# The last down product as seven block products, its weight sums made by paced DMAs

## The chip, the cores and the metric

The kernel runs on one core of a Trainium2 chip. The metric is the device time of one execution in microseconds (us). Three runs of the kernel before gave 3523.32, 3526.65 and 3530.71 us; the median is 3526.65 us. All times below are of this kernel before the change.

## The reference

Three transformer blocks run one after the other on a sequence of 1024 positions with 1024 features, all in fp32. Each block has a mixing part and a feed-forward part (f1, f2, f3 below). What matters here is the feed-forward part of the third block and what stands around it:

```python
mod = jax.nn.silu(c) @ w_ada + b_ada          # six vectors of 1024: shifts, scales, gates
x = x + gate1 * rms_norm_3(mix, norm1_post)   # mix: spatial gating and pools, times w_out
h = rms_norm_3(x, norm2_pre) * (1.0 + scale2) + shift2
f = jnp.square(jax.nn.relu(h @ w_fc1)) @ w_fc2   # 1024 -> 4096 -> 1024
x = x + gate2 * rms_norm_3(f, norm2_post)
```

`f` is a product of 1024 x 4096 activations with a 4096 x 1024 weight. It is called the down product of f3.

## The kernel before, in words

Activations lie feature-major: `X[half]` holds 8 tiles of 128 features by 512 positions, for two halves of the positions. Every product of a weight tile with an activation tile is three TensorE matmuls (`mm3`), since both operands are split into a high part and a remainder (`hi`/`lo`, `Hh`/`Hl`): high by high, high by low, low by high. The high part is written by ScalarE (`whi<-raw`, `Hh<-raw`), the remainder by VectorE (`wlo<-raw,whi`, `Hl<-raw,Hh`).

The weights come as one stream (`Stream`): `load` (L183) issues a DMA of up to 512 KB on SyncE's queue into one of the `raw` buffers, `_split` makes high part and remainder of it in a slot, and the products take the slots in the order of the stream. `tick` is called after every few matmuls; it splits the next weight when its load is old enough by the kernel's own count of matmul time (`self.pe`).

The up products (`up7`) already use Strassen's scheme with seven products (in Winograd's form). Their results go through `relu2` on ScalarE and by a DMA on its queue to a DRAM tensor `gdf`. `start` fetches one of the seven partial results back by a DMA on GpSimd's queue.

The down product of f3 (`down7`) goes over the 4096 hidden features in nine chunks of two or four tiles of 128 (`CHUNKS`). For each chunk and each of 8 output tiles and 2 halves it accumulates in PSUM, and VectorE adds the sum to `X` (`X<-X,mm`). The last chunk works in pieces of 512, 256 and 256 positions (`PARTS`). Then `tail` takes the mean of squares (`ax<-ones,acc`), spreads the reciprocal root over the partitions by a small matmul (`row_bcast`: `ax<-ident,rr`), scales (`X<-X,gp,ax`), adds the residual `xr` and sends the result out.

What stands between the products runs as background generators next to them: the norm after f2 (`norm2_gen`), the pools of block 3 (`ax<-w,wpl`, a chain of four window sizes, each built from the one before by GpSimd's shift-and-add on `w`), spatial gating (`ax<-ws,vg`), the norm after the output product o3 (`post`, then `norm_gen`), and the vectors of `mod`. For each of their 48 columns `ada_unit` (L634) forms products of `w_ada` and `silu(c)` by eight VectorE instructions, and `ada_flush` sums them over the partitions with a matmul `ax<-ones,ada`.

Two things set the order. The Python code emits instructions with these generators stepped by `self.pe`. Then the Tile framework schedules them when the program is built: each engine gets one fixed list, from an estimate of what is ready when. On the chip each engine goes through its list in that order; an instruction whose operands are not there holds back those behind it on the same engine.

Of the kernel before, what the change touches and what calls it, by code (L numbers as in the profile page):

```python
# [57 lines left out]

def _feat(a):

    return np.ascontiguousarray(a.T.reshape(KT, P, a.shape[0]).transpose(1, 0, 2))


def lay_out(i):
# [42 lines left out]
    a["w3_down"] = i["w_fc2_3"].reshape(32, P, D)  # L107
# [40 lines left out]
class Stream:  # L148
# [5 lines left out]
    def __init__(self, k):  # L154
# [6 lines left out]
        self.raws = []  # L161
        self.groom = [False, False]
# [40 lines left out]
    def _split(self):  # L203
# [38 lines left out]
        while self.nd < min(self.ns + 2, len(self.seq)):  # L242
# [23 lines left out]


class Kern:
    def __init__(self, tc, a, out):
# [7 lines left out]
        self.adap = None  # L277

# [44 lines left out]
    def mm(self, out, l, r, s, e, grp=False):  # L323
        self.nc.tensor.matmul(out, l, r, start=s, stop=e, skip_group_check=grp)  # L324
# [326 lines left out]

    CHUNKS = {"f1": [2, 2] + [4] * 7, "f2": [2] + [4] * 5, "f3": [2, 2] + [4] * 7}

# [4 lines left out]
    def setup(self):  # L658
# [46 lines left out]
        def ffn7(n, up, down, with_ada=0):  # L705
# [19 lines left out]
            S[n + "h"], S[n + "d"] = [], []  # L725
            gd = S[n + "x"] = self.drp.tile([a[down].shape[0], P, T], F32, name="gd" + n)
# [168 lines left out]
    def up7(self, name):  # L895
# [3 lines left out]
        gated = name == "f2"  # L899
# [7 lines left out]
        def relu2(dst, src, m, t, scale=1.0):  # L907
            self.act(dst, src, AF.Relu, scale=scale)
            self.act(dst, dst, AF.Square)
            nc.scalar.dma_start(out=gd[m, :, 512 * t:512 * t + 512], in_=dst)  # L910
# [12 lines left out]
        for g in range(0, M, 2):  # L923
# [7 lines left out]
            for i in (0, 1):  # L931
# [7 lines left out]
                else:  # L939
                    relu2(s, ps[i], 2 * (g + i), 0)  # L940
# [7 lines left out]
        def slot():  # L948
            n[0] += 1
            return X1[:, (n[0] - 1) % 8]  # L950
# [6 lines left out]
        def start(g):  # L957

            ca = wide() if gated else None
            s1 = None  # L960
            if g < M:
                s1 = scratch() if gated else slot()
                nc.gpsimd.dma_start(out=s1, in_=sd[g])
                if gated:
                    nc.gpsimd.dma_start(out=ca[:, :512], in_=cd[g])
            return s1, ca

        nxt = start(0)
        for g, G in enumerate(groups):
# [18 lines left out]
            if g >= M:  # L988
# [4 lines left out]
                else:  # L993
                    relu2(slot(), z, 2 * g, 0)
# [11 lines left out]
            if not gated:  # L1006
                relu2(c22, c22, 2 * g + 1, 1)
# [4 lines left out]
            else:  # L1012
                relu2(c21, c21, 2 * g + 1, 0)
# [9 lines left out]
            else:  # L1023
                relu2(v, v, 2 * g, 1)
        W.groom[1] = True
        self.ext_es.close()
        self.open_ss()

    def down7(self, name, add, tail, quarters=False):
# [4 lines left out]
        residual = 0 if name == "f3" else 4  # L1034
# [478 lines left out]
    def block2(self):  # L1513
# [243 lines left out]

        self.up7("f2")
# [268 lines left out]
    def block3(self):  # L2027
# [204 lines left out]
        self.hp, e = self.pool("hp2", 1, None, "right")  # L2232
        self.ffn_es.insert(0, e)
        ac = []

        def add(m, part, ps, first, last):
            half, c0, c1 = part
            o = c0 - half * 512
            x = self.X[half][:, m, o:o + c1 - c0]
            if first:  # L2240
# [84 lines left out]
```

## Time and profile before

| | |
|---|---|
| time, median of 3 | 3526.65 us (3523.32 to 3530.71) |
| profiled execution | 3526.44 us |
| its span | 3524.6 us |
| TensorE clock granted, mean share | 0.983 |
| PE busy | 3419.4 us (97%), 16725 instructions |
| VectorE / ScalarE / GpSimd busy | 62% / 39% / 10% |
| DMA | 421.46 MB, mean 120 GB/s |

PE is TensorE, DVE VectorE, ACT ScalarE, POOL GpSimd, SP SyncE. The span is from the first to the last instruction of the profiled execution; 1.84 us of that execution lie around it. A row such as "L324 MATMUL mm<-Hh,whi" names the line of the helper, the operation, the tile written and the tiles read. PE, at 97%, is the engine whose idle stretches are to be looked for.

### The profile page before, as it was taken

What the parts mean: (1) busy time and instruction counts of PE and PEld (TensorE: products, weight loads), DVE (VectorE), ACT (ScalarE), POOL (GpSimd) and SP (SyncE); (2) the same over time, 40 slices, a digit from 0 to 9 for tenths busy, and PEclk for the clock granted to TensorE, in tenths of its full rate; (3) what the DMA queues carried; (4) which work ended last, traced back from release to release, by engine and by line L of the source; (5) the groups of instructions that cost most, each with busy time, mean ns of one, the idle gap of its engine ahead of it and who ended that gap; (6) DMA issues with size and microseconds to landing.
All of it is one profiled execution on the core that took longest, in us unless ns stands there. A gap on an engine that the chain in (4) does not pass through costs nothing. (4 is left out here: it accounts for less than half of the span.)

```text
span 3524.6 us, 43683 instructions
## 1 busy us (share of the span) xinstructions
PE 3419.4 (97%) x16725; PEld 2808.1 (80%) x16725; DVE 2201.8 (62%) x3747; ACT 1367.4 (39%) x2046; POOL 335.8 (10%) x368
## 2 busy tenths in 40 slices
PE   7999999999999989999999999999999999999998
PEld 7788898887888777876698788878778878877887
DVE  5456366556666574667768988867665676645444
ACT  3432244444112443555634444431332564451111
POOL 0111020000000210000020000000232410000003
PEclk9999999999999999998999999999999999999999
DMA  3111444336633186444325322274222154343222
GB/s 106 48 43 47 148 135 148 117 118 191 184 133 113 58 196 173 123 129 147 110 94 166 116 84 84 96 221 149 88 67 90 62 184 149 132 167 114 96 84 72
DMA packets 180964, 421.46 MB, mean 120 GB/s; under 512 B 18088, under 2 KB 58744, under 8 KB 180628
## 3 DMA queue, kind: packets, MB, share of 16 engines
q1 hardware_dynamic: 133044, 325.34, 28.8%
q10 hardware_dynamic: 38304, 67.13, 5.1%
q0 software_dynamic: 9408, 26.22, 3.6%
q8 instruction: 131, 2.15, 0.3%
q14 instruction: 77, 0.63, 0.1%
HBM read 304.50 MB, written 105.63 MB: 116 GB/s over the span
## 5 line engine op out<-in xcount | busy, mean ns | idle before, releaser
L324 PE MATMUL mm<-Hh,whi 128*128 128x512 f32 (+3 forms) x3632 | 1384.2, 381 | 11.7 <-DVE X L305 4.5
L324 PE MATMUL mm<-Hh,wlo 128*128 128x512 f32 (+3 forms) x3632 | 1365.6, 377 | 4.7 <-DVE wlo L305 4.7
L324 PE MATMUL mm<-Hl,whi 128*128 128x512 f32 (+3 forms) x3632 | 1369.6, 377 | 0.2 <-DVE Hl L305 0.2
L324 PEld LDWEIGHTS mm<-Hh,whi 128*128 128x128 f32 x3632 | 686.0, 189 | 155.3 <-issue 6.8
L324 PEld LDWEIGHTS mm<-Hh,wlo 128*128 128x128 f32 x3632 | 685.7, 189 | 138.5 <-DVE wlo L305 9.0
L324 PEld LDWEIGHTS mm<-Hl,whi 128*128 128x128 f32 x3632 | 686.1, 189 | 127.7 <-issue 1.4
L319 ACT ACTIVATE whi<-raw 128x1024 fp32r<-128x1024 f32 (+3 forms) x386 | 379.0, 992 | 694.6 <-PE mm L324 459.9
L305 DVE TENSOR_TENSOR wlo<-raw,whi 128x1024 fp32r<-128x1024 f32 (+3 forms) x386 | 441.7, 1151 | 193.3 <-ACT whi L319 182.8
L305 DVE TENSOR_TENSOR X<-X,mm 128x512 f32<-128x512 f32 (+1 forms) x446 | 290.3, 655 | 366.7 <-PE mm L324 362.1
L324 PE MATMUL mm<-t,whi 128*128 128x512 f32 x1296 | 408.6, 396 | 2.4 <-ACT whi L319 2.4
L324 PEld LDWEIGHTS mm<-t,whi 128*128 128x128 f32 x1296 | 242.9, 188 | 62.4 <-ACT whi L319 3.3
L324 PE MATMUL mm<-t,wlo 128*128 128x512 f32 x648 | 256.7, 396 | 1.9 <-DVE wlo L305 1.7
L319 ACT ACTIVATE Hh<-raw 128x1024 fp32r<-128x1024 f32 x86 | 89.6, 1057 | 364.8 <-PE mm L324 213.3
L321 ACT ACTIVATE X<-X 128x512 f32<-128x512 f32 (+1 forms) x226 | 151.9, 673 | 186.2 <-DVE X L310 153.7
L305 POOL TENSOR_TENSOR acc<-acc,sq 128x256 f32<-128x256 f32 (+1 forms) x108 | 115.9, 1074 | 910.0 <-ACT sq L321 906.4
L305 DVE TENSOR_TENSOR raw<-raw 128x512 f32<-128x512 f32 x216 | 145.2, 687 | 79.5 <-DMA raw<-in_w_up 77.1
L324 PEld LDWEIGHTS mm<-t,wlo 128*128 128x128 f32 x648 | 121.8, 188 | 33.4 <-DVE wlo L305 4.1
L305 DVE TENSOR_TENSOR Hl<-raw,Hh 128x1024 fp32r<-128x1024 f32 x86 | 104.6, 1222 | 56.9 <-ACT Hh L319 56.3
L310 DVE SCALAR_TENSOR_TENSOR ada<-raw,silc,ada 128x128 f32<-128x128 f32 x336 | 115.5, 350 | 8.3
L324 PE MATMUL mm<-whi,Hh 128*128 128x264 f32 (+4 forms) x336 | 111.7, 342 | 6.5 <-ACT Hh L319 2.8
L324 PE MATMUL mm<-wlo,Hh 128*128 128x264 f32 (+4 forms) x336 | 111.2, 340 | 2.4 <-DVE wlo L305 2.4
L310 DVE SCALAR_TENSOR_TENSOR X<-mm,X 128x512 f32<-128x512 f32 x108 | 74.5, 690 | 61.6 <-PE mm L324 60.1
(290 smaller groups left out, 3400.0 us busy)
## 6 DMA issues: line engine op xcount, KB each, us to landing
raw<-in_w_up SPq DMA_DIRECT2D x136, 512.0 KB
raw<-gdf SPq DMA_DIRECT2D x86, 512.0 KB
raw<-in_w_down SPq DMA_DIRECT2D x86, 512.0 KB
gdf<-X ACTq DMA_DIRECT2D x108, 256.0 KB
raw<-in_w_ada SPq DMA_DIRECT2D x48, 512.0 KB
gdf<-X ACTq DMA_DIRECT2D x22, 512.0 KB
B<-qd SPq DMA_DIRECT2D x36, 256.0 KB
A<-qd SPq DMA_DIRECT2D x36, 256.0 KB
```

Source lines behind the costliest of these rows:

```text
L305: eng.tensor_tensor(out=out, in0=a, in1=b, op=op)
L310: self.nc.vector.scalar_tensor_tensor(out=out, in0=a, scalar=s, in1=b, op0=op0, op1=op1)
L319: self.nc.scalar.activation(out, in_, f, scale=scale, **kw)
L321: self.nc.scalar.activation(out, in_, f, bias=bias, scale=scale, **kw)
L324: self.nc.tensor.matmul(out, l, r, start=s, stop=e, skip_group_check=grp)
```

## The change

The rows and columns of f3's down weight are laid out as blocks (four groups of hidden features, by four quarters of the matrix, `_quarters`). The 4096 x 1024 weight and the hidden activations are cut into 2 x 2 blocks, and the product is made of seven block products of 512 x 2048 x 512 instead of eight (`down_parts`). Four of the seven need sums of weight blocks. These are made in DRAM, by 32 DMAs of 1 MB on GpSimd's queue: 16 plain copies into `sw` and 16 that add to it (`sums`). They are spread out from the start of the up product of f2 (`up7("f2")`) by a pace of 24.0 on `self.pe`. Each waits for the last matmul that the source has emitted before it. The up product of f3 writes the seven pieces of the hidden activations that the products need: four more VectorE operations and four DMA writes on GpSimd's queue per group. The weight stream of the down product gets both operands of each product from DRAM; the residual `xr` comes in by two GpSimd DMAs into `Hh` at its start. The last part of `tail` is one of 512 positions.

The core of the diff:

```diff
     def tick(self):
         self.k.ada_flush()
+        self.k.sums_step()
     def mm(self, out, l, r, s, e, grp=False):
-        self.nc.tensor.matmul(out, l, r, start=s, stop=e, skip_group_check=grp)
+        self.last_mm = self.nc.tensor.matmul(out, l, r, start=s, stop=e, skip_group_check=grp)
+    def sums(self, name, w, pace, at=None):
+        S = self.S[name + "s"]
+        for i, q in ((0, 1), (1, 0), (2, 1), (3, 2)):
+            for e in range(4):
+                self.sums_todo.append((S[i, 2 * e:2 * e + 2], w[e, q], {}))
+        for i, q in ((0, 3), (1, None), (2, 0), (3, None)):
+            for e in range(4):
+                r = slice(2 * e, 2 * e + 2)
+                src = w[e, q] if q is not None else S[i - 1 if i == 1 else 1, r]
+                self.sums_todo.append((S[i, r], src, dict(accum_op=ALU.add, max_dma_last_dim=4096)))
+    def sums_step(self):
+        if self.sums_todo and self.pe >= self.sums_at:
+            dst, src, kw = self.sums_todo.pop(0)
+            ins = self.nc.gpsimd.dma_start(out=dst, in_=src, **kw)
+            self.tc.add_manual_dep(
+                ins.ins, self.last_mm.ins.name,
+                mybir.DependencyInfo(mybir.DependencyClass.Sync, mybir.DependencyReason.DATA),
+                reason="sums")
+            self.sums_at = self.pe + self.sums_pace
+    ORDER = ("P1", "P2", "P6", "P7", "P4", "P5", "P3")
...
+    def down_parts(self, name, out, tail):
+        W.ahead = 4
+        for n, i in enumerate(self.ORDER):
+            if new:
+                ps = [self.ps() for _ in range(4)]
+            for e in range(8):
+                wa, wb = (W.get(u) for u in D_[8 * n + e])
+                for m in range(4):
+                    for k in (0, 1):
+                        self.mm3(ps[m], wa.hi[:, w], wa.lo[:, w], wb.hi[:, x], wb.lo[:, x], ...)
...
+        self.sums("f3", a["w3_down"], 24.0)
         self.up7("f2")
...
+                if parts:
+                    relu2(v, v)
+                    t1_, t2_, t4_ = slot(), slot(), slot()
+                    self.tt(t1_, ca, v, ALU.subtract)
+                    self.tt(v, c22, v, ALU.subtract)
+                    self.stt(t2_, t1_, -1.0, c22, ALU.mult, ALU.subtract)
+                    self.stt(t4_, t2_, -1.0, c21, ALU.mult, ALU.subtract)
+                    for i, t in ((3, t1_), (5, v), (4, t2_), (6, t4_)):
+                        nc.gpsimd.dma_start(out=piece(i, g), in_=t)
...
+        xr = self.Hh.bitcast(F32)
+        for k in (0, 4):
+            nc.gpsimd.dma_start(out=xr[:, k:k + 4, :T], in_=self.xd[:, k:k + 4])
...
-        self.down7("f3", add, tail, quarters=True)
+        self.down_parts("f3", out, tail)
```

With the 32 DMAs in the program the framework arrives at other lists, also where the source is the same. Three places follow, all on TensorE; numbers behind a name tell tiles apart.

In the down product of f2 the five sums of columns of `mod` stood apart, with 36 to 84 matmuls between each and the next (here the first of them):

```order
L324 MATMUL mm_19031<-Hl_87,whi_18935 128x512
L324 MATMUL mm_19031<-Hh_86,wlo_18936 128x512
L324 MATMUL ax_19045<-ones_60,ada_18959 128x1
L324 MATMUL mm_19052<-Hh_86,whi_18804 128x512
L324 MATMUL mm_19052<-Hl_87,whi_18804 128x512
L324 MATMUL mm_19052<-Hh_86,wlo_18805 128x512
```

Now the five stand in a row, ahead of 24 matmuls that the first of them stood behind (`mm_19026` is the `mm_19006` of before):

```order
L337 MATMUL mm_19008<-Hl_87,whi_18954 128x512
L337 MATMUL mm_19008<-Hh_86,wlo_18955 128x512
L337 MATMUL ax_19065<-ones_60,ada_18979 128x1
L337 MATMUL ax_19129<-ones_60,ada_19040 128x1
L337 MATMUL ax_19197<-ones_60,ada_19104 128x1
L337 MATMUL ax_19243<-ones_60,ada_19172 128x1
L337 MATMUL ax_19386<-ones_60,ada_19300 128x1
L337 MATMUL mm_19026<-Hh_86,whi_18823 128x512
L337 MATMUL mm_19026<-Hl_87,whi_18823 128x512
```

The fifth sum, which had 192 matmuls between the first and itself, now stands ahead of all of them.

In the third block's pools, each window's products (`wpl`, from buffer `w0` or `w1`) had 60 to 84 matmuls of another product between them and those of the next window; here is the second window:

```order
L324 MATMUL mm_20966<-Hl_87,whi_20844 128x512
L324 MATMUL mm_20966<-Hh_86,wlo_20845 128x512
L324 MATMUL ax_20979<-w0_20738,wpl_20740 128x512
L324 MATMUL ax_20982<-w0_20738,wpl_20740 128x512
L324 MATMUL mm_20966<-Hh_86,whi_20844 128x512
```

Now they stand behind that whole product, with 12 matmuls from the second window to the third (shown) and 12 from the third to the fourth:

```order
L337 MATMUL ax_21008<-w0_20765,wpl_20767 128x512
L337 MATMUL mm_21422<-Hh_86,whi_21135 128x512
L337 MATMUL mm_21444<-Hh_86,whi_21217 128x512
L337 MATMUL mm_21466<-Hh_86,whi_21301 128x512
L337 MATMUL mm_21422<-Hl_87,whi_21135 128x512
L337 MATMUL mm_21422<-Hh_86,wlo_21136 128x512
L337 MATMUL mm_21444<-Hl_87,whi_21217 128x512
L337 MATMUL mm_21444<-Hh_86,wlo_21218 128x512
L337 MATMUL mm_21466<-Hl_87,whi_21301 128x512
L337 MATMUL mm_21466<-Hh_86,wlo_21302 128x512
L337 MATMUL mm_21489<-Hh_86,whi_21405 128x512
L337 MATMUL mm_21489<-Hl_87,whi_21405 128x512
```

The rest of the twelve is one more matmul, and then come the products of the third window.

At the end of the output product o3, the sums and broadcasts of the norms stood between its matmuls, from here on:

```order
L324 MATMUL mm_21782<-Hl_87,whi_21678 128x256
L324 MATMUL mm_21782<-Hh_86,wlo_21679 128x256
L324 MATMUL ax_21795<-ones_60,acc_21508 128x1 x4
L324 MATMUL mm_21782<-Hh_86,whi_21678 128x256
L324 MATMUL mm_21782<-Hl_87,whi_21678 128x256
```

Now they stand behind o3's last matmul (`mm_22437`), and ahead of the first of f3's up product (`mm_22500`):

```order
L337 MATMUL mm_22437<-Hh_86,wlo_21712 128x256
L337 MATMUL ax_21828<-ones_60,acc_21540 128x1 x4
L337 MATMUL ax_21903<-ones_60,acc_21540 128x1 x4
L337 MATMUL ax_21871<-ident_59,rr_21836 128x128 x2
L337 MATMUL ax_21984<-ident_59,rr_21911 128x128 x2
L337 MATMUL ax_22037<-ones_60,acc_21540 128x1 x4
L337 MATMUL ax_22119<-ident_59,rr_22045 128x128 x2
L337 MATMUL ax_22166<-ones_60,acc_21540 128x1 x4
L337 MATMUL ax_22301<-ones_60,acc_21669 128x1 x4
L337 MATMUL ax_22249<-ident_59,rr_22174 128x128 x2
L337 MATMUL mm_22500<-Hh_86,whi_22236 128x512
```

The nine `ax` groups are the post norm and the next norm of the first half of the positions, in two parts, and the first sums of the second half; some 300 matmuls of o3 moved ahead of them.

At the end of f2's down product, likewise, the norm's broadcast (`ax<-ident,rr`), which stood 32 matmuls behind its sums (`ax<-ones,acc`), now follows them directly, and the first matmuls of the next product follow it.

## Rows read from the trace of the kernel before

**Rows 1.** The page: busy time, share of the span and instructions.
```profile
PE 3419.4 (97%) x16725; PEld 2808.1 (80%) x16725; DVE 2201.8 (62%) x3747; ACT 1367.4 (39%) x2046; POOL 335.8 (10%) x368
```
**Rows 2.** Busy time by stretch: columns named in its second row, of f3.
```profile
core 0: us, PE busy (x) PEld busy (x) DVE busy (x) ACT busy (x) POOL busy (x), PEclk, DMA share, GB/s
2890.00:3160.00 270.00, 267.97 (x1150) 215.29 (x1149) 153.39 (x199) 128.89 (x184) 4.31 (x8) 1.00 0.44 149
3160.00:3200.00 40.00, 38.76 (x166) 30.46 (x165) 26.51 (x31) 16.84 (x20) 0.00 (x0) 1.00 0.53 175
3200.00:3450.00 250.00, 250.00 (x1079) 202.07 (x1078) 108.29 (x132) 41.85 (x41) 0.00 (x0) 1.00 0.26 85
...
3150.00:3155.00 5.00, 5.00 (x22) 3.75 (x20) 0.00 (x0) 0.40 (x1) 0.00 (x0) 1.00 1.04 413
```
**Rows 3.** Costliest groups, f3's down product: count | busy us, mean ns | idle before.
```profile
L305 DVE TENSOR_TENSOR X<-X,mm 128x512 f32<-128x512 f32 x90 | 61.4, 686 | 128.6 <-PE mm L324 128.6
L305 DVE TENSOR_TENSOR wlo<-raw,whi 128x1024 fp32r<-128x1024 f32 x22 | 26.5, 1223 | 5.8 <-ACT whi L319 5.8
```
**Rows 4.** The page's costliest groups, f3's up product.
```profile
L310 DVE SCALAR_TENSOR_TENSOR X<-mm,X 128x512 f32<-128x512 f32 x108 | 74.5, 690 | 61.6 <-PE mm L324 60.1
```
**Rows 5.** DMA issues: KB each, median us to landing.
```profile
X<-xd POOLq DMA_DIRECT2D x8, 1024.0 KB, 13.7
```
**Rows 6.** The timeline, end of f3: start, length, instruction, idle before it.
```profile
3495.77 1.30 POOL L305 TENSOR_TENSOR X<-X,xr 128x512 f32<-128x512 f32 x1
3509.51 0.73 POOL L305 TENSOR_TENSOR X<-X,xr 128x256 f32<-128x256 f32 x1 [0.63 <-DVE X L310]
3520.37 0.44 DVE L305 TENSOR_TENSOR X<-X,xr 128x256 f32<-128x256 f32 x1
```
**Rows 7.** The timeline, f2's down product, PE, SP and DVE.
```profile
2373.44 0.28 PE L324 MATMUL ax<-ones,ada 128*128 128x1 f32 x2
2385.76 0.33 SPq L183 DMA_DIRECT2D raw<-in_w_ada  x1
2390.30 0.28 DVE L314 TENSOR_SCALAR ada<-raw,silc 128x128 f32<-128x128 f32 x1
2393.02 0.73 DVE L310 SCALAR_TENSOR_TENSOR ada<-raw,silc,ada 128x128 f32<-128x128 f32 x2
```
**Rows 8.** The timeline, end of f2's down product, PE and DVE.
```profile
2522.22 4.84 PE L324 MATMUL ax<-ones,acc 128*128 128x1 f32 x30 [1.42 <-ACT acc L321]
2531.84 0.69 DVE L305 TENSOR_TENSOR X<-X,mm 128x512 f32<-128x512 f32 x1 [4.06 <-PE mm L324]
2537.21 1.16 PE L324 MATMUL ax<-ident,rr 128*128 128x128 f32 x8 [0.79 <-DVE rr L305]
2540.81 0.74 DVE L310 SCALAR_TENSOR_TENSOR Hl<-nt,mod,Hh 128x512 fp32r<-128x512 f32 x1
```
**Rows 9.** The timeline, third block's pools, PE and POOL.
```profile
2631.92 1.88 PE L324 MATMUL ax<-w,wpl 128*128 128x512 f32 x4
2640.29 0.22 POOL L305 TENSOR_TENSOR w<-w,zb 128x16 f32<-128x16 f32 x1
```
**Rows 10.** The timeline, o3's norms, PE and DVE.
```profile
2769.03 0.95 PE L324 MATMUL ax<-ones,acc 128*128 128x1 f32 x8
2798.87 0.16 DVE L305 TENSOR_TENSOR rr<-rr,rt 128x2 f32<-128x2 f32 x1
2800.77 0.61 PE L324 MATMUL ax<-ident,rr 128*128 128x128 f32 x4
```
**Rows 11.** The chain that ended last, behind the second half's sums: start, us.
```profile
2566.26 10.86 PE mm L324 x35
...
2578.01 54.07 PE mm L324 x233
```
**Rows 12.** Busy time by stretch, behind the second half's sums.
```profile
2566.00:2571.00 5.00, 5.00 (x14) 3.94 (x14) 2.80 (x13) 1.49 (x2) 0.00 (x0) 0.50 0.29 105
```

More of the change, by code (lines that the diff above doesn't have):

```diff
@@ L241, in _split @@
         self.ns += 1
-        while self.nd < min(self.ns + 2, len(self.seq)):
+        while self.nd < min(self.ns + self.ahead, len(self.seq)):
             self.load()
@@ L1027, in up7 @@
         self.open_ss()
+    def down_parts(self, name, out, tail):
+        W = self.W
+        D_ = self.S[name + "d"]
+        sp, e = self.pool("sums", 1, None, "right")
+        self.ffn_es.insert(0, e)
+        s = sp.tile([P, 4, 512], F32, name="s_")
+        v = sp.tile([P, 4, 512], F32, name="v_")
+        W.ahead = 4
+        new = True
+        for n, i in enumerate(self.ORDER):
+            if n == 6:
+                self.drop_raws()
+                W.ahead = 2
+            if new:
+                ps = [self.ps() for _ in range(4)]
+            for e in range(8):
+                wa, wb = (W.get(u) for u in D_[8 * n + e])
+                for m in range(4):
+                    for k in (0, 1):
+                        w, x = slice(k * 512 + m * P, k * 512 + m * P + P), slice(k * 512, k * 512 + 512)
+                        self.mm3(ps[m], wa.hi[:, w], wa.lo[:, w], wb.hi[:, x], wb.lo[:, x],
+                                 new and e == 0 and k == 0, e == 7 and k == 1, not new)
+                    if m == 3:
+                        W.done(wa)
+                        W.done(wb)
+                    if e == 7:
+                        z = ps[m]
+                        if i == "P1":
+                            self.act(s[:, m], z, AF.Copy)
+                        elif i == "P2":
+                            out(0, m, z, 1)
+                        elif i == "P6":
+                            self.tt(v[:, m], z, s[:, m], ALU.add)
+                        elif i == "P7":
+                            self.tt(s[:, m], z, s[:, m], ALU.add)
+                        elif i == "P4":
+                            out(0, 4 + m, z, -1, s[:, m])
+                        elif i == "P5":
+                            out(1, 4 + m, z, -1, s[:, m])
+                        else:
+                            out(1, m, z, 1, v[:, m])
+                    W.tick()
+                    if m % 2:
+                        self.step()
+                    else:
+                        self.fine()
+            new = i not in ("P1", "P6", "P5")
+            if i == "P4":
+                self.unsummed = True
+                self.norms[0] = self.bg(tail((0, 0, 512)))
+            elif i == "P3":
+                self.unsummed = True
+                self.norms[1] = self.bg(tail((1, 512, 1024)))
     def down7(self, name, add, tail, quarters=False):
@@ L2270, in tail @@
             self.unsummed = False
-            if half and len(xr) < 2:
-                t = self.hp.tile([P, KT, 512], F32, tag="h0", name="xr")
-                self.dma(t, self.xd[:, :, 512:])
-                xr.append([t[:, k] for k in range(KT)])
             yield self.after(1.0)
```

100 lines of the change are left out of this document (57 added, 43 removed).

## The prediction

> **What bounds the kernel now.** I read the page's first part first: PE is busy for 97% of the span and no other engine for more than 80% [rows 1]. Then the busy time by stretch, for the part that the change rewrites. In f3's down product PE is busy in 250.00 of 250 us [rows 2], so one instruction less there is its full duration less, and a matmul of 512 columns stands for 250 / 1079 = 0.232 us. In the stretch of f3's up product and the transition to the down product PE was idle for 2.0 + 1.2 us [rows 2]. VectorE there is the engine that waits: before its adds to X it sat idle for 128.6 us, all of it for PE [rows 3]. So whatever makes PE wait anywhere in the program shows in the time, and whatever only loads VectorE or the queues shows where the cover runs out. The change does one thing to PE in f3, and through the framework's new lists another thing to PE far from f3. So I followed the lists, and then the timeline at the places where they differ.
>
> **What f3's down product gives.** Before: 28 tiles of hidden features by 8 output tiles by 2 halves by 3 products are 1344 matmuls of 512 columns; the last chunk has 96 of 512 and 192 of 256. After: 7 block products of 192, that is 1344. The 96 and 192 go: 96 x 0.232 + 192 x 0.116 = 44.5 us, all on the path, since PE has no idle time there. The transition's 3.3 us of idle I count as gone as well, since both operands now come as a stream with four units loaded ahead (bounds 0 and 3.3).
>
> What has to keep up: 112 loads of 512 KB in 1344 x 0.232 = 312 us, or 188 GB/s. The densest stretch of before moved 413 GB/s with PE busy in 5.00 of 5 us [rows 2]. VectorE has 112 remainders at 1.223 us [rows 3], 137 us, and most of its 0.686 us adds are gone. Neither is a bound, so I charge 0; if each of the 56 pairs of operands came half a microsecond late, 28 us.
>
> f3's up product gets four more VectorE operations of about 0.690 us [rows 4] in each of 16 groups, 44 us in all. VectorE is busy there for 153 of 270 us [rows 2]; with them it is 73%. I charge 2 us, for the places where a group's results are wanted at once; bounds 0 and 8 (44 with no cover at all).
>
> The end of the kernel: the last part of the norm was 256 positions, and now it is 512. GpSimd's add takes 1.30 instead of 0.73 us [rows 6], and some eight pairs of such operations, shared by two engines, lie behind the last matmul: 8 x 0.57 = 4.6 less what overlaps, 4 us (bounds 2 and 8).
>
> So f3 by itself: -44.5 - 3.3 + 2 + 4 = -41.8 us.
>
> **The sums.** 32 DMAs of 1 MB stand on GpSimd's queue, one about every 24 us. The only DMA of that size on that queue in before, which also adds, took a median of 13.7 us to land [rows 5], so one is done before the next is due. Behind each stands GpSimd's other work, its waits being for matmuls that PE reaches anyway. I charge the transfers nothing (bounds 0 and 32 x 1 us = 32, if each delays one load that PE waits for).
>
> [...]
>
> **What the new lists cost.** PE takes its list in order. Four groups of small matmuls (`ax`) used to stand among large ones, so that the VectorE chain before each ran under cover. Now the cover stands behind or ahead of them.
>
> 1. f2's down product: five column sums in a row. The first stood at 2373.44 [rows 7]; the place where all five stand now is 24 matmuls ahead of that, about 2367.9. The last needs a column whose `w_ada` load was issued at 2385.76, whose chain began at 2390.30 and ended at 2393.02 + 0.73 = 2393.75 [rows 7]. That load waits for a raw buffer, which VectorE frees by splits that do not need PE to go on; so it is hardly earlier than before. PE then stands from 2367.9 to about 2391 to 2394. I take 22 us, with bounds of 12 (the load goes as soon as the first chains are done) and 30 (it is late as well).
>
> 2. The end of f2's down product: sums at 2522.22 with 4.84 us, the broadcast at 2537.21, so 10.2 us lie between, in which VectorE waited 4.06 us for matmuls only because an add to X stood in its list [rows 8]. Some 6 us of bare chain remain, and from the broadcast to the first finished operand of the next product it is 2540.81 + 0.74 - 2537.21 = 4.3 us [rows 8]. Both were covered and now are not: 10 us (7 to 16).
>
> 3. The pools: from a window's product to GpSimd's last operation for the next window it is 2640.29 + 0.22 - 2631.92 = 8.6 us [rows 9]. Cover is now the product itself, 1.88 us, and 12 matmuls, 2.8 us. Three such links are open by 3.9 us each, 12 us (8 to 20).
>
> 4. o3's norms: from the first sums at 2769.03 to the last VectorE operation before the broadcast of the second part, 2798.87 + 0.16, it is 30.0 us [rows 10]. Before, that chain ran under 300 matmuls of o3. Now the sums start when o3 has ended, and f3's first matmul stands behind that broadcast. The other norms' small operations run in the same time. Some waits inside the chain for PE's own list go: 29 us (24 to 34).
>
> PE also comes back slowly from a stall. [...] Place 2 had it before; for places 1, 3 and 4 I take 7 us (0 to 11). The waits that before had at place 2 (1.42 and 0.79 [rows 8]) are part of the new ones: -2.
>
> [...]
>
> **The sum.** -41.8 + 22 + 10 + 12 + 29 + 7 - 2 = +36.2 us on the profiled execution's 3526.44 us, which is 0.2 us from the median: 3562.6, say 3563 us.
>
> **Rivals.**
>
> A. The lists look worse than they run. The four chains run on engines that are otherwise idle during the stall, and the loads come earlier since VectorE is not held up. Then place 1 costs 8, 2 and 3 cost 4 each and 4 costs 14 (half of its chain was VectorE work for others), without a clock loss: -41.8 + 30 - 2 = -13.8, 3513 us, faster. For it: VectorE was idle for 4.06 us of the chain at place 2 only for PE's sake. Against it: at place 4 the chain is as long as VectorE's own work. It decides when the four places together with the clock cost less than 42 us.
>
> B. The down product is bound by its operands. Loads, two splits and the product form one chain per pair; the residual's 4 MB come at its start on the same DMA engines. At half a microsecond per pair, +28: 3591 us. For it: each pair covers only 24 matmuls, 5.6 us. Against it: four units ahead, and 413 GB/s seen.
>
> C. The sums hold GpSimd's queue. `start` of f2's up product gets its partial results over that queue, and GpSimd does half of the norms' adds; at 1 us for each of 32, +32: 3595 us. For it: 13.7 us per accumulating transfer, and more under load. Against it: 24 us between them.
>
> D. Both sides cancel, within 0.2% (7 us, about what a measurement of this kernel can tell from no change). Nothing in the trace makes the two sides equal; it is only the ground between A and the forecast.
>
> **How the numbers follow.** Forecast 0.66, A 0.12, B 0.10, C 0.08, D 0.04. The forecast's own range, from the bounds of its four places and the clock, is 3535 to 3585. To hold the time 8 times in 10 the range goes down to 3522, over D's ground to the edge of A, and up to 3598, over B and C. Slower: 0.66 + 0.10 + 0.08 = 0.84; same 0.04; faster 0.12.
>
> **What would show it.** In the page after, PE's busy time falls by about 40 us while the span grows. Five `ax<-ones,ada` stand in one row of PE's timeline with a wait of some 20 us before the last, for VectorE's `ada`. The groups `ax<-ident,rr` and `ax<-w,wpl` carry waits for VectorE and GpSimd that before did not have, some 30 us of them between o3 and f3's first up matmul. f3's down product shows PE busy throughout, in about 312 us. I am wrong if PE waits for whi, wlo, Hh or Hl there (B), if GpSimd's DMA results release PE in f2's up product (C), or if the idle time of PE at the four places is under 42 us in all (A).

## The result and the profile after

The changed kernel takes 3658.85 us (median of 4 runs, 3650.31 to 3666.53), the kernel before 3528.57 in the same series: a ratio of 1.0371, interval 1.0345 to 1.0397. It is slower, as forecast, but by 130 us, and the forecast was 36; the time lies outside the range.

The first part of the page after, which answers to [rows 1]:

```profile
span 3656.7 us, 43357 instructions
PE 3418.6 (93%) x16437; PEld 2792.1 (76%) x16437; DVE 2220.3 (61%) x3725; ACT 1412.7 (39%) x2079; POOL 397.1 (11%) x468
```

PE has 288 instructions less and is as long busy as before (3419.4 us). Most of what the removed matmuls gave, the clock took: the granted mean is 0.96 where it was 0.983, and it is low in the stretches in which PE waits (shown at the end of the part on why). A run told of below, product_alone, has the same 16437 matmuls without the lists moved ahead of f3; there they are busy for 3380.9 us at a granted 0.981. PE's idle time went from 105 to 238 us.

I divided both executions at milestones that both have (a norm's broadcast, an `ada` sum, the first and last matmul of f3's down product). The list of after has 7.2 us of large matmuls more ahead of the milestone between places 2 and 3, and 2.6 us more ahead of the one between place 4 and f3; these are put back where they were. The last column is the same difference between two experiments that are told of below; ahead of f3 PE's lists differ there nearly as those of before and after do (the list of tiny_sums is that of before but for 31 places).

| stage | forecast, us | before to after, us | tiny_sums to quarter_sums, us |
|---|---|---|---|
| up to the norm ahead of f2 | 0 | +6.9 | +2.6 |
| f2's up product | 0 | +26.7 | +27.6 |
| place 1, five ada | +24.3 | +31.6 | +36.7 |
| place 2, end of f2 | +8.0 | +21.6 | +25.8 |
| place 3, pools | +14.3 | +34.0 | +31.7 |
| place 4, o3's norms | +31.3 | +35.5 | +35.4 |
| f3's up product | +2.0 | +20.9 | +1.1 |
| f3's down product | -47.8 | -51.1 | |
| tail | +4.0 | +6.0 | -2.0 (with the down product) |
| sum | +36.2 | +132.1 | +158.8 |

The first row I put down to scatter: PE's list is the same up to there in eleven of the kernels, and in their profiled executions the norm broadcast that ends it came between 1819.1 us (the kernel before) and 1826.1 us (the changed one).

**Place 1.** PE's timeline (start, length, instruction, idle time before it and its releaser), f2's down product, for [rows 7]:

```profile
2401.53 0.28 PE L337 MATMUL ax<-ones,ada 128*128 128x1 f32 x2
2408.30 0.58 PE L337 MATMUL ax<-ones,ada 128*128 128x1 f32 x2 [6.49 <-DVE ada L323]
2416.18 0.58 PE L337 MATMUL ax<-ones,ada 128*128 128x1 f32 x2 [7.29 <-DVE ada L323]
2419.21 0.59 PE L337 MATMUL ax<-ones,ada 128*128 128x1 f32 x2 [2.45 <-DVE ada L323]
2433.02 0.58 PE L337 MATMUL ax<-ones,ada 128*128 128x1 f32 x2 [13.22 <-DVE ada L323]
```

The five stand in a row and the last comes 31.5 us after the first, with 29.5 us of waiting. The first of the 24 large matmuls behind them in the list started at 2434.45 us, 32.92 us after the first sum; in before, where it stood ahead of that sum, it started 5.56 us before it (2367.88 against 2373.44). The forecast had the mechanism and its size within its bounds.

**Place 2.** PE's timeline at the end of f2, for [rows 8]:

```profile
2619.04 6.99 PE L337 MATMUL ax<-ones,acc 128*128 128x1 f32 x32 [13.63 <-POOL acc L318]
2633.64 2.07 PE L337 MATMUL ax<-ident,rr 128*128 128x128 f32 x8 [7.61 <-DVE rr L318]
2637.37 0.80 PE L337 MATMUL mm<-whi,Hh 128*128 128x512 f32 x1 [1.67 <-ACT Hh L334]
```

The second and third wait were forecast (10 us). The first was not, and GpSimd's and SyncE's timelines tell where it comes from:

```profile
2600.15 0.88 POOL L684 DMA_DIRECT2D swf<-in_w_down  x1 [25.87 <-PE mm L337]
2600.75 1.59 POOL L318 TENSOR_TENSOR acc<-acc,sq 128x512 f32<-128x512 f32 x1
2612.87 0.45 POOL L318 TENSOR_TENSOR ws<-ws,tril 128x128 f32<-128x128 f32 x1 [10.53 <-DMA tril<-in_tril]
2613.28 1.26 POOL L318 TENSOR_TENSOR acc<-acc,sq 128x512 f32<-128x512 f32 x1
2617.73 1.25 POOL L318 TENSOR_TENSOR acc<-acc,sq 128x512 f32<-128x512 f32 x1
```

```profile
2572.95 22.45 SPq L341 DMA_DIRECT2D xd<-X  x3
2606.98 0.48 SPq L341 DMA_DIRECT2D tril<-in_tril  x1
```

A small load, `tril`, is issued at 2606.98 behind the stores of X; it lands at 2612.87; and an operation of the spatial gating that needs it (`ws<-ws,tril`) now stands in GpSimd's list ahead of adds to the norm's `acc`, for which PE waits. In before all four of them stood behind the adds. The two lists there, before and after (lines of before numbered by its own source):

```
before: L305 TENSOR_TENSOR acc<-acc,sq 128x512
        L305 TENSOR_TENSOR ws<-ws,tril 128x128 x4
after:  L318 TENSOR_TENSOR acc<-acc,sq 128x512
        L318 TENSOR_TENSOR ws<-ws,tril 128x128
        L318 TENSOR_TENSOR acc<-acc,sq 128x512
        L318 TENSOR_TENSOR ws<-ws,tril 128x128
```

**Places 3 and 4**, PE's timeline, for [rows 9] and [rows 10]:

```profile
2803.30 2.08 PE L337 MATMUL ax<-ws,vg 128*128 128x128 f32 x8 [5.58 <-DVE zb L327]
2817.47 2.08 PE L337 MATMUL ax<-w,wpl 128*128 128x512 f32 x2 [1.25 <-POOL w L318]
2828.61 1.98 PE L337 MATMUL ax<-w,wpl 128*128 128x512 f32 x4 [1.68 <-POOL w L318]
...
2932.64 3.58 PE L337 MATMUL ax<-ones,acc 128*128 128x1 f32 x16 [6.92 <-POOL acc L318]
2947.96 1.87 PE L337 MATMUL ax<-ones,acc 128*128 128x1 f32 x8 [8.32 <-POOL acc L318]
2954.93 1.19 PE L337 MATMUL ax<-ident,rr 128*128 128x128 f32 x4 [5.10 <-DVE rr L318]
```

The chains are open where the forecast had them. The three links at the pools (`w`) wait less than the 3.9 us forecast for each; but there are waits at the other small matmuls of the pools, 5.58 us for `zb` the longest, and at the first product after the norm, and the granted clock is 0.93, where before it was 1.00. The stretch from the end of place 2 to the end of place 3 (us, then busy PE, PEld, DVE, ACT, POOL, granted clock, DMA share, GB/s):

```profile
2671.00:2881.00 210.00, 187.76 (x795) 146.36 (x794) 93.26 (x122) 58.95 (x84) 48.39 (x48) 0.93 0.34 89
```

PE is idle for 22 us of it. In before it was busy for 183.00 of 183 us there, at a clock of 1.00, and did 30 matmuls more.

**f2's up product**, which the forecast held to be unchanged, PE's, ScalarE's and VectorE's timelines:

```profile
1907.77 1.65 PE L337 MATMUL mm<-t,whi 128*128 128x512 f32 x3 [9.16 <-ACT t L332]
1986.96 0.50 PE L337 MATMUL mm<-Hh,whi 128*128 128x512 f32 x1 [4.06 <-DVE X L318]
2055.22 0.80 PE L337 MATMUL mm<-Hh,whi 128*128 128x512 f32 x1 [4.65 <-ACT X L332]
```

```profile
1906.66 4.46 ACT L332 ACTIVATE t<-X 128x1024 fp32r<-128x1024 f32 x4 [2.43 <-DVE X L323]
```

```profile
1901.73 2.62 DVE L318 TENSOR_TENSOR raw<-raw 128x512 f32<-128x512 f32 x4 [4.73 <-DMA raw<-in_w_up]
1905.41 4.63 DVE L323 SCALAR_TENSOR_TENSOR X<-X,X 128x1024 f32<-128x1024 f32 x4
```

Before, the six `t` tiles were written early (ScalarE's instructions on `t`, with the first and last start, and PE's first product with one):

```profile
L319 ACT ACTIVATE t<-X x6: 1047/1052/1064, 1861.6 to 1875.5; 128x1024 fp32r<-128x1024 f32 x6
1891.54 0.63 PE L324 MATMUL mm<-t,whi 128*128 128x512 f32 x2
```

Here large matmuls changed places, not small ones: where before 24 products with a `t` tile are followed by 12 with Hh and Hl, 48 with `t` now stand in a row. PE comes to the first of them at the same place of its list as before. It is the `t` tiles that are late. Before, ScalarE had begun the last of them at 1875.5, 16 us ahead of PE; now it writes four of six in one go from 1906.66 on, when PE already stands. They wait for four VectorE operations on X, which now stand in VectorE's list behind sums of weight tiles (`raw<-raw`) that wait for a load. So the lists of ScalarE and VectorE had moved as well, and the forecast had not looked at them.

**f3**, busy time by stretch (for [rows 2]), and PE's longest-lasting wait in its up product (us in all, times, longest):

```profile
3000.00:3320.00 320.00, 302.98 (x1271) 237.59 (x1272) 217.67 (x299) 149.95 (x222) 52.91 (x90) 0.99 0.55 187
3320.00:3634.00 314.00, 314.00 (x1369) 254.92 (x1368) 158.72 (x147) 123.86 (x135) 31.94 (x24) 1.00 0.60 201
```

```profile
PE mm L337 <- DVE X L318: 12.9, 16, 1.6
```

The down product is busy from end to end and takes 314 us (forecast 312); its operands never come late. The 16 waits for X in the up product are not one for each of its 16 groups: on PE's timeline they stand between 3093 and 3225 us, one to three in a group, and the last five groups have none. Before, none of PE's waits in that product was for X. Large matmuls have changed places in this product too (runs of 24 and 12 with `t` became runs of 30 and 6), so the waits can come from the four added operations or from the new order; no run tells the two apart.

### The profile page after: what moved, and what is told of

It reads as the page before. It is cut to its first block, busy times and chain, and to the rows that moved or that the text cites. A ratio compares the mean times of both kernels' runs of the same rounds, so it can differ in the third digit from the quotient of the medians.

```text
span 3656.7 us, 43357 instructions
## 1 busy us (share of the span) xinstructions
PE 3418.6 (93%) x16437; PEld 2792.1 (76%) x16437; DVE 2220.3 (61%) x3725; ACT 1412.7 (39%) x2079; POOL 397.1 (11%) x468
## 4 chain that ended last, share of the span: by engine, by line
PE 47%; DVE 10%; DMA 5%; ACT 3%; issue 2%; POOL 1%; SPq 0%; ACTq 0%; DVEq 0%; POOLq 0%
PE mm L337 40%; PE ax L337 5%; PE o L337 2%; DVE X L323 2%; DVE X L318 1%; DMA raw<-in_w_up 1%; DVE wlo L318 1%; DMA raw<-in_w_ada 1%; DMA cb<-cs 1%; DVE raw L318 1%; POOL acc L318 1%; ACT X L334 1%; DVE ca L323 1%; DVE acc L318 0%; DMA raw<-gdf 0%
## 5 line engine op out<-in xcount | busy, mean ns | idle before, releaser
L337 PE MATMUL mm<-Hh,whi 128*128 128x512 f32 (+3 forms) x3088 | 1179.9, 383 | 28.7 <-DVE X L318 14.5
L337 PE MATMUL mm<-Hl,whi 128*128 128x512 f32 (+3 forms) x3088 | 1168.3, 378 | 1.0 <-DVE Hl L318 0.8
L337 PE MATMUL mm<-Hh,wlo 128*128 128x512 f32 (+3 forms) x3088 | 1163.1, 377 | 6.0 <-DVE wlo L318 6.0
L318 DVE TENSOR_TENSOR wlo<-raw,whi 128x1024 fp32r<-128x1024 f32 (+3 forms) x466 | 546.0, 1183 | 404.9 <-ACT whi L332 402.4
L337 PEld LDWEIGHTS mm<-Hh,whi 128*128 128x128 f32 x3088 | 586.6, 190 | 156.4 <-DVE X L318 19.9
L337 PEld LDWEIGHTS mm<-Hl,whi 128*128 128x128 f32 x3088 | 586.4, 190 | 109.2 <-DVE Hl L318 2.4
L318 POOL TENSOR_TENSOR acc<-acc,sq 128x512 f32<-128x512 f32 (+1 forms) x102 | 115.5, 1135 | 650.4 <-ACT sq L334 639.9
L337 PE MATMUL mm<-whi 128*128 128x512 f32 x448 | 177.0, 395 | 0.0
L337 PE MATMUL mm<-whi,wlo 128*128 128x512 f32 x448 | 176.4, 394 | 0.0
L337 PE MATMUL mm<-wlo,whi 128*128 128x512 f32 x448 | 175.8, 393 | 0.0
L337 PEld LDWEIGHTS mm<-t,wlo 128*128 128x128 f32 x648 | 122.3, 189 | 35.4 <-DVE wlo L318 6.0
```

What stands on the lines that cost most here:

```text
L318: eng.tensor_tensor(out=out, in0=a, in1=b, op=op)
L337: self.last_mm = self.nc.tensor.matmul(out, l, r, start=s, stop=e, skip_group_check=grp)
```

## The experiments

Theory L: the moved lists cost, because on PE, or on an engine that feeds it, instructions now stand where their operands are late. Theory D: the transfers cost, through their traffic and through what stands behind them on GpSimd's queue. Theory Q: GpSimd's waits cost. All ratios are to the kernel before, on the same chip, with 95% intervals.

**Which part of the change.** product_alone leaves the sums out and lets P5, P6, P7 and P3 read plain blocks:

```diff
-                A.update({"P5": sw[0], "P6": sw[1], "P7": sw[2], "P3": sw[3]})
+                A.update({i: [a[down][e // 2, q, e % 2] for e in range(8)]
+                          for i, q in (("P5", 1), ("P6", 0), ("P7", 1), ("P3", 2))})
...
-        self.sums("f3", a["w3_down"], 24.0)
```

> The changed kernel without the sums: four of the seven block products read a plain block of the weight where they would read a sum, so the output is another. All lists up to f3's up product are those of the kernel before. Theories L and Q: f3's down product 51 us shorter, the tail 6 us longer, f3's up product 13 to 18 us longer through its four new operations: 3495 to 3505 us. Theory T: slower than the kernel before, over 3540 us.

3496.18 us, 0.9915 (0.9898 to 0.9932). sums_alone is the kernel before with the 32 sums and their waits, whose results nothing reads:

> The kernel before, with only the 32 sums and their waits put in; nothing reads what they write. Theories L and Q: everything up to f3's up product is as late as in the changed kernel, 130 to 160 us, while f3 stays as it was, so 3660 to 3690 us. Theory T (the cost lies in f3's new loads and pieces): within 10 us of the kernel before.

3687.80 us, 1.0451 (1.0434 to 1.0469). The product gives 30 us and the sums take 162, together a loss of 132 us, where the change measured 130.

**Is it the waits?** lists_no_wait keeps every engine's list and takes the wait from the sums alone:

```diff
-                mybir.DependencyInfo(mybir.DependencyClass.Sync, mybir.DependencyReason.DATA),
+                mybir.DependencyInfo(mybir.DependencyClass.NoSync, mybir.DependencyReason.DATA),
```

> The changed kernel with the 32 sums told to the scheduler as before (a dependency that orders, without a semaphore), so that every engine's list is the same, but on the chip none of them waits for a matmul. Theory L (the new lists cost it): the time stays at 3640 to 3665 us, with the five column sums, the pools and o3's norms as far apart as in the changed kernel (stage costs 32, 27 and 38 us). Theory Q (a sum that waits holds GpSimd's list): the start of f2's up product loses most of its 27 us and the end of f2 its wait of 13.6 us for GpSimd's acc adds; the time falls to 3605 to 3625 us.

3695.56 us, 1.0476 (1.0460 to 1.0491): 37 us slower than with the waits. The two waits that Theory Q should have removed are still there, 9.0 us for `t` in f2's up product (9.16 with the sums' waits) and 14.7 for `acc` at the end of f2 (13.63). Without waits the sums crowd: the longest took 42.8 us to land, against 22.4 in the changed kernel, and PE has a new wait of 27.3 us for VectorE's X in f2's up product. That the waits cost no more than 6 us on nearly the old lists, tiny_sums shows below. no_dependency takes the dependency out before the lists are made, and they come out differently again, with the sums early:

```diff
-            self.tc.add_manual_dep(
...
-                reason="sums")
```

> The changed kernel without the sums' dependency on a matmul at all. The scheduler then puts all 32 at the front of GpSimd's list, in block 1, and moves small matmuls in block 1 and at the end of f1, while everything from block 2 on stands as before. Theory L: 30 to 120 us over the 3496 us without sums, lost in block 1 and f1's down product: 3525 to 3615 us. Theory D: the same loss as in the changed kernel, 3640 us or more.

3688.57 us, 1.0461 (1.0439 to 1.0483), above what L had (3525 to 3615) and in the range of D. PE's idle time is now mostly between 300 and 700 and between 1000 and 1600 us; the sums are issued between 1 and 1362 us, and some 2400 places of PE's list ahead of f3 hold another matmul than before, more than I had counted on. sums_in_f1 starts them at f1's up product:

```diff
+        self.sums("f3", self.a["w3_down"], 24.0)
         self.up7("f1")
...
-        self.sums("f3", a["w3_down"], 24.0)
         self.up7("f2")
```

> The changed kernel with its sums started at f1's up product instead of f2's, same pace and same waits. The lists from f2's up product to f3's up product are those of the kernel before. Theories L and Q: as without sums, plus at most 10 us from waits in f1 and block 2: 3495 to 3515 us. If what counts is the sums' traffic or their number (theory D): 3560 us or more.

3683.31 us, 1.0445 (1.0429 to 1.0460). My expectation was off by 170 us, since I had thought of f1 as a place with room. The four places of the changed kernel lost nothing here; f1's down product and the block behind it did, PE's small matmuls waiting 53.8 us for VectorE's `ada` and 59.7 for its `ca`. So the places themselves are not at fault: the sums move the lists around wherever they are put.

**Fewer and closer.** All 32 with 12 us between them from the start of f2's up product (all_in_f2_up), 16 in f1's and 16 in f2's up product at 4 us (two_bursts), and 12, 12 and 8 in those of f1, f2 and f3 at 8 us (three_bursts):

```diff
-        self.sums("f3", a["w3_down"], 24.0)
+        self.sums("f3", a["w3_down"], 12.0, self.pe + 0)
         self.up7("f2")
```

and for two_bursts, with a function that takes so many of the sums from the list:

```diff
+        self.sums_part(16, 4.0, 0)
         self.up7("f1")
...
-        self.sums("f3", a["w3_down"], 24.0)
+        self.sums_part(16, 4.0, 0)
         self.up7("f2")
```

> The changed kernel with a pace of 12 instead of 24, so that all 32 sums fall into f2's up product. Of the moved groups only the five column sums in f2's down product are left; the norms, the pools and the end of f2 stand where they stood before. Theory L: as without sums, 3496 us, plus that group's 32 us and up to 27 us at the start of f2's up product: 3525 to 3560 us. Theory D: 3620 us or more.

> As three_bursts, but 16 from the start of f1's and 16 from the start of f2's up product, at a pace of 4. TensorE's small matmuls stand where they stood before. Theory L: 3495 to 3520 us; the denser bursts may delay a few loads. Theory D: 3600 us or more; and since the transfers are twice as dense, no faster than three_bursts by more than 5 us.

> The changed kernel with the same 32 sums, each still waiting for its matmul, but in three bursts at a pace of 8: 12 from the start of f1's up product, 12 from f2's, 8 from 60 behind the start of f3's. TensorE's small matmuls then stand in every product ahead of f3's down product where they stood before. Theory L (the new lists cost it): as without sums, 3496 us, plus at most 20 for denser transfers: 3495 to 3516 us. Theory D (the sums' traffic or their place on GpSimd's queue costs it wherever they are): 3600 us or more.

3569.19 us (1.0119, 1.0103 to 1.0134), 3585.13 (1.0166, 1.0150 to 1.0181) and 3603.90 (1.0218, 1.0203 to 1.0234). All three are faster than the changed kernel, and fewer small matmuls are moved in them: the group of five `ada` sums in all_in_f2_up, none in the other two. But each burst still cost 30 to 53 us in its up product against product_alone, and the two without a moved small matmul are slower than the one with a group. All three lie above what L had, three_bursts in the range of D. I took the rest for traffic at first. In the lists, though, large matmuls of those up products had moved too, so these three runs could not tell L from D.

**Lists or transfers.** That took a kernel with the same lists and less to transfer. quarter_sums has each sums DMA moved only a quarter of its rows; PE's list is the changed kernel's, instruction for instruction (the product reads plain blocks, as above). tiny_sums cuts them to 2 of 128 rows, and there PE's list comes out nearly as before's, small matmuls within 9 places. The edit of quarter_sums (tiny_sums has 2 for 32):

```diff
-            ins = self.nc.gpsimd.dma_start(out=dst, in_=src, **kw)
+            ins = self.nc.gpsimd.dma_start(out=dst[:, :32], in_=src[:, :32], **kw)
```

> The changed kernel, each sums DMA cut to a quarter of its rows (256 KB where it was 1 MB; 32 of them at the same places, each with its wait), and the product reads plain blocks where it read sums, so that its output is not the reference's. TensorE's list is the changed kernel's, instruction for instruction. Base: product_alone, 3496 us. Theory L (the small matmuls moved to places where their operands are late cost most: about 125 of the 162 us between product_alone and the changed kernel, and that doesn't depend on what the transfers carry): 3610 to 3650 us, with waits for POOL acc, DVE ada and DVE rr near those of the changed kernel (36.9, 29.5, 22.1 us). Theory D (the traffic of the sums, and what stands behind them on GpSimd's queue while they move it): a quarter of 162, so 3525 to 3555 us, and these waits under half.

> The changed kernel, each sums DMA cut to 16 KB (2 of 128 rows), the 32 issues and their waits kept, the product on plain blocks (output not the reference's). TensorE's small matmuls then stand within 9 matmuls of where the kernel before has them. Theories L and D both: 3494 to 3512 us, as product_alone (3496.2). Theory W (the waits themselves, 21 sums that wait at the head of GpSimd's list with the loads and adds behind them, are what costs): 3530 us or more, with the 13 to 18 us of acc adds at the end of f2 still late.

quarter_sums 3662.69 us, 1.0386 (1.0370 to 1.0401); tiny_sums 3502.30 us, 0.9924 (0.9908 to 0.9941). PE's waits in the changed kernel, in quarter_sums and in tiny_sums (us in all, times, longest):

```profile
PE ax L337 <- POOL acc L318: 36.9, 9, 13.6
PE ax L337 <- DVE ada L323: 29.5, 4, 13.2
PE ax L337 <- DVE rr L318: 22.1, 6, 7.6
```

```profile
PE ax L337 <- POOL acc L318: 40.6, 9, 18.7
PE ax L337 <- DVE ada L323: 34.1, 4, 17.8
PE ax L337 <- DVE rr L318: 20.8, 6, 7.6
```

```profile
PE ax L337 <- DVE rr L318: 8.5, 5, 4.2
PE ax L337 <- POOL acc L318: 6.8, 6, 2.0
```

Three quarters of the bytes gone, and nothing gained (13 us more than the upper end that L had); 32 issues with their waits, on nearly the old lists, and nothing lost beyond 6 us against product_alone. So neither the bytes nor the waits of the sums are what costs in the changed kernel. One thing quarter_sums does not take away: a sum of 256 KB did not land sooner than one of 1 MB (median 11.3 us, longest 26.5; 8.3 and 22.4 in the changed kernel). How long the sums stand in the queue is therefore not tested here, but by late_in_f2_up below. The granted clock differs with the lists, 0.93 and 0.78 against 1.00 and 0.87 in what follows. First two stretches of quarter_sums, and then those of tiny_sums in which PE goes through the same places of its list (us, busy PE, PEld, DVE, ACT, POOL, then granted clock, DMA share, GB/s):

```profile
1900.00:2000.00 100.00, 85.89 (x342) 66.12 (x343) 81.68 (x95) 35.21 (x35) 8.72 (x16) 0.93 0.36 119
2600.00:2700.00 100.00, 65.41 (x276) 52.76 (x274) 46.63 (x94) 42.33 (x62) 30.44 (x29) 0.78 0.17 49
```

```profile
1894.76:1977.29 82.53, 80.52 (x344) 63.91 (x343) 71.65 (x86) 31.60 (x31) 7.50 (x14) 1.00 0.43 135
2532.06:2602.82 70.76, 65.97 (x275) 53.84 (x276) 45.75 (x94) 38.72 (x58) 27.19 (x22) 0.87 0.21 66
```

For the same places of the list quarter_sums takes 100 us where tiny_sums takes 82.53 and 70.76, with its DMA engines no busier (0.36 and 0.17 against 0.43 and 0.21). quarter_in_f2_up does to all_in_f2_up what quarter_sums does to the changed kernel:

> all_in_f2_up (pace 12 from the start of f2 up; 3569.2 us, 73 over product_alone; only the group of five ada sums moved) with each sums DMA cut to a quarter of its rows, the product on plain blocks (output not the reference's). TensorE's list: the same one group moved. If that group costs what its waits show (22.7 us of ada there) and the rest, about 50 us, is traffic: 3525 to 3540 us. If traffic is all of it: 3510 to 3518. If traffic is none of it: 3560 to 3570.

3579.81 us, 1.0151 (1.0136 to 1.0166), no faster than with whole sums (3569.19). I had expected 50 us of traffic there; three quarters of the bytes less saved nothing. (Here, too, the smaller sums landed no sooner, at a median of 11.8 us against 8.5.)

**Whole transfers on lists that stay.** late_in_f2_up starts the whole sums 150 us into f2's up product, about 8 us apart; of PE's list only the group of place 1 moves. in_f3_up has them 60 us into f3's up product, 2 us apart by the source's count, and moves 94 large matmuls there. Both compute all of the result. The edit of late_in_f2_up:

```diff
-        self.sums("f3", a["w3_down"], 24.0)
+        self.sums("f3", a["w3_down"], 7.0, self.pe + 150)
```

> The changed kernel with its 32 sums of 1 MB whole, but begun 150 us into f2's up product, one about every 7 us. TensorE's list is product_alone's but for one group, the five ada sums in f2's down product (place 1): f2's up product, the end of f2, the pools, o3's norms and all of f3 stand as there. Theory L (only the moved lists cost): tiny_sums 3502 + about 37 for place 1 = 3533 to 3545 us, PE waits for DVE ada 20 to 35 us and no loss at the other places. Theory D (traffic, and GpSimd's loads behind it, cost as well when the sums come whole and close together, 32 MB written and as much read in some 220 us): 3560 us or more, PE idle for over 20 us in f2's up product.

> The 32 sums of 1 MB whole, begun 60 us into f3's up product, one about every 2 us by the source's own count. All lists up to there are product_alone's; in f3's up product 94 large matmuls change places, behind it none. Theory L: 3502 + up to 27 (what the moved large matmuls cost in f2's up product) = 3502 to 3530 us, that is before or a little less. Theory D: the sums take 32 x 8 us or more of the 250 us left of f3's up product, whose loads come over the same queue, and the third block product wants the first of them 90 us into the down product: 3550 us or more, with PE waiting for GpSimd's loads in f3's up product, or for wlo and whi at P6.

late_in_f2_up: 3533.40 us, 1.0017 (1.0008 to 1.0027), where L had 3533 to 3545. Two of its stretches and its wait:

```profile
2100.00:2200.00 100.00, 100.00 (x432) 80.74 (x431) 78.48 (x88) 41.39 (x44) 8.27 (x12) 1.00 0.74 197
2200.00:2300.00 100.00, 94.99 (x401) 75.51 (x401) 77.54 (x86) 43.34 (x48) 8.83 (x10) 0.99 0.92 209
```

```profile
PE ax L337 <- DVE ada L323: 23.1, 4, 9.6
```

In the first stretch the DMA engines are busy for 74% and PE for 100%, in the second for 92% and 95%. The median is 31 us over that of tiny_sums; of the 26 us between the two profiled executions, 25.6 are lost at place 1. This settles the transfers: whole sums, landing in 8.5 us at the median, cost next to nothing where PE's list stays (0.4 of the 26 us). L is shown, and D and Q are not what costs in the changed kernel, where the sums are further apart.

in_f3_up: 3592.75 us, 1.0176 (1.0157 to 1.0194), and here D had the time right:

```profile
2900.00:3000.00 100.00, 68.44 (x252) 52.45 (x250) 39.99 (x57) 24.48 (x35) 19.58 (x35) 0.83 0.82 283
3000.00:3100.00 100.00, 64.89 (x228) 48.27 (x228) 43.78 (x63) 24.39 (x36) 21.94 (x32) 0.83 1.05 249
```

```profile
PE mm L337 <- DVE X L318: 59.6, 19, 12.3
DVE X L318 <- DMA X<-sdf: 22.1, 2, 11.7
```

PE waits for X, and VectorE in its turn for f3's own loads: for `X<-sdf` on GpSimd's queue, where the sums stand ahead of it, and for weights on SyncE's queue (14.1 us the longest, 3.4 in product_alone). So the transfers cost here, with the 32 issued within 173 us (2901.2 to 3074.1): 22.1 us of VectorE's waiting is for `X<-sdf`. In late_in_f2_up, with the 32 within 263 us, all but 0.4 of the 26 us were lost at place 1; on the changed kernel's list, with the 32 within 1024 us, a quarter of the bytes saved nothing (3662.69 against 3658.85 us). The share of the DMA engines alone doesn't tell the two apart: PE was busy for 68% at a share of 0.82 here and for 95% at 0.92 in late_in_f2_up. What the 94 moved matmuls add here, no run shows.

No version that computes the result was faster than before; late_in_f2_up is 0.2% from it. A list with that start of the sums and the old place 1 would, by tiny_sums, be near 3502; none of those that were built had it.

## Why the prediction was right and wrong

1. **f3's down product** (-47.8): right, -51.1. Rival B (late operands) is out: PE was busy in 314.00 of 314 us.
2. **f3's up product** (+2, bounds 0 to 8): mis-sized, +20.9; product_alone, with the old lists ahead of it, has +17.7 there. 12.9 us are the 16 waits for X, 0.8 us each on average, between 3093 and 3225 us. I compared VectorE's load with the stretch (73% busy) and neither the chain of one group, whose results PE wants at once, nor the order of the list. Which of the two made X late stays open.
3. **The sums at nothing** (0 to 32): right for the transfers themselves at this spacing. Rival C is out: in f2's up product of the changed kernel no wait of PE is for a load on GpSimd's queue, and late_in_f2_up sends whole sums there at under a third of the spacing (263 us for the 32 against 1024), with 0.4 of 26 us lost outside place 1. What the sums did cost, they cost through the lists.
4. **Place 1** (+22, 12 to 30) and **place 4** (+29, 24 to 34): mechanism and size right; 31.6 and 35.5 include a stretch at a lower granted clock each. Behind place 1's last sum it was 0.58 (2434 to 2439 us), with eight matmuls about 0.43 us apart, and 1.00 from 2444 on, with matmuls 0.23 us apart; in place 4's chain it was 0.50 (2932 to 2960), and 0.77 where f3's first matmuls follow (2966 to 2976).
5. **Place 2** (+10, 7 to 16): mechanism half right, +21.6. I followed PE's list and VectorE's chain, and left out that GpSimd's list had changed as well: adds to `acc` now stand behind an operation that waits 10.53 us for `tril`. (In lists_no_wait, where no sum waits ahead of it, that operation waits for `tril` as well, and PE's wait stays.)
6. **Place 3** (+12, 8 to 20): mis-sized, +34.0. I priced the three links between windows, which measured 4.4 us of waiting in all, and not the other waits in the stretch (22 us of idle time with them) nor its clock (0.93).
7. **The step that failed**: "Four groups of small matmuls (`ax`) used to stand among large ones". I took moved small matmuls on PE's list for all that the new lists do, and priced f2's up product at nothing. There 224 positions of PE's list hold another large matmul than before, ScalarE and VectorE write the `t` tiles only when PE already stands, and that cost 26.7 us, which quarter_sums against tiny_sums repeats at 27.6. Rival A (lists cheaper than they look) erred to the other side: it had 30 us for the four places, and 122.7 were measured.
8. **Clock** (+7): too small. No run shows the 7 us by itself. The rows of before have 35 matmuls at 0.310 us each and the 233 behind them at 0.232 [rows 11], at a granted 0.50 early among the 35 [rows 12]: 2.7 us, at place 2. What the runs show in place of the 7 us is this: the same matmuls are busy for 3418.6 us in the changed kernel and for 3380.9 in product_alone, 38 us apart, so the sign that PE's busy time falls by about 40 us failed as well. Stretches of the changed kernel show the granted clock at 0.83, 0.73 and 0.78:

```profile
2400.00:2500.00 100.00, 69.70 (x294) 56.28 (x293) 51.32 (x108) 12.12 (x12) 1.76 (x2) 0.83 0.55 152
2600.00:2700.00 100.00, 67.85 (x267) 54.39 (x266) 52.68 (x102) 46.82 (x68) 33.64 (x31) 0.73 0.23 57
2900.00:3000.00 100.00, 66.56 (x385) 59.47 (x384) 53.96 (x140) 49.45 (x120) 40.52 (x51) 0.78 0.22 75
```

Of the 96 us between forecast and result, 27 are f2's up product, 20 place 3, 19 f3's up product, 14 place 2, 11 places 1 and 4, 7 the scatter at the front; the down product and the tail make up the rest, -1. The range was also added up wrongly: the bounds of the four places and the clock give 3534 to 3594 us and not 3535 to 3585; the result lies above both.

What stays open is why the lists move. From the lists alone: with sums of 16 KB they hardly move, with 256 KB they move just as with 1 MB, and without sums not at all. That speaks for the scheduler's own estimate of a transfer and not for the wait in the source; no run here shows it.

## What to carry to other kernels

A piece of background work is to be priced first by what it does to the order of everything else: compare the lists of all engines, large instructions as well as small, before and after. To tell the order from the load, keep the lists and shrink the load, and then keep the load and restore the lists; here a quarter of the bytes cost as much as all of them (3662.69 and 3658.85 us), and all of them, with only place 1 moved, next to nothing outside it (0.4 of 26 us). Look, too, whether the smaller load is really over sooner; here it was not (11.3 against 8.3 us). A chain on which PE waits is priced by the latest of all engines that feed it, GpSimd's list and SyncE's small loads among them: at place 2 PE's longest wait, 13.63 us, came from those two.

## What was not expected of the hardware

Waits on GpSimd's queue were worth having: with the same lists, the kernel whose transfers were held back by a matmul each took 3658.85 us, 37 us less than the one whose transfers were let go at once (3695.56). And beside the 32 MB of DRAM-to-DRAM transfers, half of them adding, PE was busy in late_in_f2_up for 100 of 100 us in a stretch where the DMA engines' share was 0.74, and for 95 where it was 0.92 (in_f3_up, where they came closer together: 68 at 0.82 and 65 at 1.05). In quarter_sums a transfer of 256 KB in 32 of 128 rows took no less time to land than one of 1 MB in all rows in the changed kernel: 11.3 against 8.3 us at the median.
